# Seven half-sized products for 36 gate-and-up pairs of the second layer (Strassen's identity)

## The chip, the cores and the metric

The kernel runs on one NeuronCore of one Trainium2 chip. The metric is device time in microseconds (us) of one execution; the time given for a kernel is the median of its runs. The profile is of one execution of its own.

TensorE (PE) multiplies a stationary tile of 128 x 128 weights with a moving operand of up to 512 columns and accumulates in PSUM, eight banks of 512 fp32 columns each. PEld is TensorE's weight load, DVE is VectorE, ACT is ScalarE, POOL is GpSimd, SP is SyncE, which only issues transfers here.

## What is computed

A decoder trunk of two layers on 512 tokens of 1024 channels, in fp32. Each layer has three sub-layers, every one with an RMSNorm and a modulation from the conditioning vector: a feed-forward block, a token mixer of three head groups, and a second feed-forward block. Only the feed-forward blocks matter here:

```
def swiglu(h, w_in, w_out):
    gate, up = jnp.split(h @ w_in, 2, axis=-1)
    return (jax.nn.silu(gate) * up) @ w_out

h = modulate(rms_norm(x, norm_g[l, 2]), sh2, sc2)
x = x + FFN_HALF * gt2[:, None, :] * swiglu(h, ffn2_in[l], ffn2_out[l])
```

w_in is 1024 x 5632 (2816 gate and 2816 up columns), w_out 2816 x 1024.

## The kernel before

Channels lie on the 128 partitions, tokens along the free dimension: x is a tile of 8 blocks of 128 channels by 512 tokens. Every fp32 operand of the large products is split in two: a high part, which an ACT copy rounds to TensorE's fp32r type, and a low part, the difference, which one subtraction stores. For the activations these are `hh` and `hl` after the norm (`norm`, lines 333 to 349; its factor `rb` lies in PSUM, x in SBUF) and `gh` and `gl` between the two products of a block; for the weights `whi` and `wlo`. A product of the two is three matmuls (`mm3`, lines 414 to 420): high times high, high times low, low times high, all added up in the same PSUM columns.

A feed-forward block (`ffn`, line 481) works in two halves of 11 pairs each. A pair is the 128 gate columns and the 128 up columns of the same index: one weight tile of 128 x 1024 for each (8 blocks of 128 x 128, along the 1024 input channels). The in-phase of a half runs over its pairs: for each of the two tiles 8 blocks x 3 matmuls of 512 columns into a bank, then `swiglu` (line 540): Silu on ACT out of PSUM, a product with the other bank on DVE, the high part on ACT, the low part on DVE. In the first half the first two pairs go together, in two rounds of 256 tokens, because the norm also comes in two halves of 256 tokens. Behind the in-phase of a half stands its out-phase: 8 output blocks of 33 matmuls each, added to x on DVE (line 426); in the second half ACT and POOL also square and add up x for the next norm (lines 291 to 306).

The weights come through one list, `Weights.units`, that `plan` (line 428) writes in the order of use. `use(i)` (line 181) first advances (line 176) two pointers: tiles up to i+2 are split, in four `whi` and four `wlo` buffers (line 170 on ACT, line 171 on DVE, for a few marked tiles on POOL), and tiles up to i+5 are requested by SP in three `wraw` buffers (line 158). A transfer is issued when its buffer is free, in the order of the list.

While the first layer runs, the 144 tiles of the modulation weights pass through six buffers `adaw` of the same pool as the feed-forward tiles (lines 249 to 260). In the second layer's blocks nothing of that is left to do.

The order of the instructions on each engine is set before the run by a scheduler that works with the order of writing as priority and with estimated times; on the chip each engine works through its list in order.

Lines that matter: 158 load, 170 and 171 high and low part of a weight tile, 418 to 420 mm3, 543 to 546 swiglu, 342 to 349 norm, 301 sums of squares on POOL, 578 to 580 and 590 to 592 and 806, 807, 873 parts of the mixer.

Of the kernel before, what the change touches and what calls it, by code (L numbers as in the profile page):

```python
# [7 lines left out]
F32 = mybir.dt.float32  # L8
# [131 lines left out]
class Weights:  # L140
# [5 lines left out]
        self.units, self.raw, self.hl = [], {}, {}  # L146
        self.nd = self.ns = 0

    def add(self, ap, width, pool=False):
        self.units.append((ap, width, pool))  # L150
        return len(self.units) - 1

    def dma_to(self, i):
        while self.nd < len(self.units) and self.nd <= i:
            ap, w, _ = self.units[self.nd]
            t = self.pool.tile([128, D], F32, name="wraw", tag="wraw", bufs=self.br)
            dst = t[:, :w] if len(ap.shape) == 2 else t[:, :w].rearrange("p (i n) -> p i n", n=ap.shape[2])
            self.nc.sync.dma_start(dst, ap)
            self.raw[self.nd] = t
            self.nd += 1  # L160

    def split_to(self, i):
        while self.ns < len(self.units) and self.ns <= i:
            j = self.ns
            self.dma_to(j)
            _, w, pool = self.units[j]
            r = self.raw.pop(j)
            h = self.pool.tile([128, D], F32R, name="whi", tag="whi", bufs=self.b)
            lo = self.pool.tile([128, D], F32R, name="wlo", tag="wlo", bufs=self.b)
            self.nc.scalar.activation(h[:, :w], r[:, :w], AF.Copy)  # L170
            (self.nc.gpsimd if pool else self.nc.vector).tensor_tensor(lo[:, :w], r[:, :w], h[:, :w].bitcast(F32),  # L171
                                                                       op=ALU.subtract)
            self.hl[j] = (h[:, :w], lo[:, :w])
            self.ns += 1

    def advance(self, i):
        n = 1 if i < KC - 1 else self.AHEAD_SPLIT
        self.split_to(i + n)
        self.dma_to(i + (n if n == 1 else self.AHEAD_DMA))

    def use(self, i):
        self.advance(i)
# [3 lines left out]
class Build:  # L186
    def __init__(self, tc, a, out, dbg=None, layers=L, stop=None):
        self.tc, self.nc, self.a, self.out, self.dbg = tc, tc.nc, a, out, dbg or (lambda *k: None)
        self.layers, self.stop = layers, stop
        self.bgq = []  # L190
        self.nbank = 0
        self.sql = {}

    def bg(self, n=1):
# [11 lines left out]
    def load_consts(self):  # L206
        nc, cp, a = self.nc, self.const, self.a
        self.ones = cp.tile([128, 128], F32, name="ones")
        nc.vector.memset(self.ones, 1.0)
        self.scratch = cp.tile([128, 1], F32, name="scratch")  # L210
        self.eps = cp.tile([128, 1], F32, name="eps")
        nc.vector.memset(self.eps, EPS)

        def ld0(key, shape, dt=F32, eng=None):
            t = cp.tile(shape, dt, name="k_" + key)
            (eng or nc.scalar).dma_start(t, a[key])
            return t

        self.ident = ld0("k_ident", [128, 128])
        self.bada = ld0("bada", [128, L, NADA * KC])  # L220
        self.ng = ld0("ng", [128, L, 3, KC])

        def late():
            def ld(key, shape, dt=F32):
                return ld0(key, shape, dt, nc.gpsimd)

            self.fng = ld("fng", [128, KC])
            self.kd = ld("k_kd", [128, 4])
            self.gc = ld("k_gc", [128, 2])
# [12 lines left out]
            self.onat = cp.tile([128, 4, 2, 256], F32, name="onat")  # L242
            self.sg = cp.tile([128, 4, 2, 256], F32, name="sg")
# [184 lines left out]
    def plan(self):  # L428
        W, a = self.W, self.a
        self.u = {}  # L430
        for l in range(self.layers):
            for which in (0, 1, 2):
                if which != 1:
# [5 lines left out]
                    for half in range(2):  # L439
                        for i in range(FH):  # L440
                            if l == 0 and w == 0 and half == 0 and i < FIRST:
                                continue
                            for s in range(2):
# [37 lines left out]
    def ffn(self, l, which):  # L481
        nc = self.nc
        w = which // 2
        gate = self.mod[l]
        gh = self.gh = self.fp.tile([128, FH, T], F32R, name="gh")
        gl = self.gl = self.fp.tile([128, FH, T], F32R, name="gl", tag="gl")
        for half in range(2):
            i = 0
            if l == 0 and which == 0 and half == 0:
# [2 lines left out]
                self.first_gl = self.last_gl  # L492
                i = FIRST
            while i < FH:
                group = [i, i + 1] if (half == 0 and i == 0) else [i]
                i += len(group)
                js = [(j, s) for j in group for s in range(2)]
# [16 lines left out]
                                     slice(None), k == 0, k == KC - 1)  # L514
                for j in group:
                    self.swiglu(j, ps[j, 0], ps[j, 1])
                self.bg(self.bg_rate * len(group))
            def out_mm(d, p, hs, last):
                for q, (k0, k1) in enumerate(((0, 6), (6, 11))):
# [16 lines left out]
                self.bg(self.bg_rate)  # L536
            if tail:
                self.halves(range(KC - tail, KC), out_mm, gate, 24 * which + 16)

    def swiglu(self, j, pg, pu):  # L540
        nc = self.nc
# [52 lines left out]
    def mixer(self, l):  # L594
# [5 lines left out]
        krot = mp.tile([128, 2, T], F32, name="krot")  # L600
        vnat = mp.tile([128, 4, 256], F32, name="vnat")
        G = mp.tile([128, 120], F32, name="G")[:, 0:96].rearrange("p (c k) -> p c k", c=4)
        onat, sg, stats = self.onat, self.sg, self.stats
        with tc.tile_pool(name="mtmp", bufs=1, reuse_waits="tile") as tp:
            self.tp = tp
# [529 lines left out]
    def open_ffn(self, ada, first=False):  # L1135
        self.fp_cm = self.tc.tile_pool(name="ffn", bufs=1, side="right", reuse_waits="tile")
        fp = self.fp = self.fp_cm.__enter__()
        self.open_sq(fp)
        if ada:
            self.cact = fp.tile([128, D], F32, name="cact")  # L1140
            if first:
# [101 lines left out]
```

## Time and profile before

| | |
|---|---|
| median of 3 runs | 2120.87 us (2117.64 to 2123.96) |
| the profiled execution's own time | 2122.84 us |
| its span, first to last instruction | 2121.1 us |
| PE busy | 2093.0 us (99%) |
| PEld busy | 1743.2 us (82%) |
| DVE busy | 1108.0 us (52%) |
| ACT busy | 796.3 us (38%) |
| POOL busy | 211.0 us (10%) |
| mean granted TensorE clock | 0.996 of 2.4 GHz |
| data moved by DMA | 269.10 MB, mean 127 GB/s |

Busy time is a union: matmuls overlap each other (each is shown some 0.39 us long where one begins every 0.23 us), so the distance of two starts is what a matmul costs. Idle time of an engine that is not the bottleneck costs nothing. In a timeline, the columns are start, length, engine, line, operation, tiles and shape, and in brackets the idle time before it and what ended it.

### The profile page before, as it was taken

How to read it: one execution, taken by the hardware profiler on the slowest of the kernel's cores; microseconds unless marked ns; L12 is line 12 of the kernel's file. 1: busy time of each engine (PE TensorE's matmuls, PEld its weight loads, DVE VectorE, ACT ScalarE, POOL GpSimd, SP SyncE). 2: the span in 40 equal slices, each digit the busy share in tenths (PEclk: the TensorE clock that was granted, in tenths of full speed). 3: DMA queues.
4: the chain of work that ended last, by engine and by line, in shares of the span. 5: the costliest groups of instructions: out<-in, count | busy, mean ns of one | idle time of the engine just before them, and what ended most of it. 6: DMA issues, size and time to landing. Idle time of an engine off the chain costs nothing.

```text
span 2121.1 us, 27803 instructions
## 1 busy us (share of the span) xinstructions
PE 2093.0 (99%) x10938; PEld 1743.2 (82%) x10938; DVE 1108.0 (52%) x1731; ACT 796.3 (38%) x1309; POOL 211.0 (10%) x196
## 2 busy tenths in 40 slices
PE   9999999999999999999999999999999999999998
PEld 7888888988965988888888888889788669888887
DVE  8894333637875799533353333335578754333332
ACT  4422323543665522222342222234527654222323
POOL 1000001312301200000110000012223020000002
PEclk9999999999999999999999999999999999999999
DMA  9894323423310699432333233235232112233322
GB/s 342 310 358 156 91 83 100 144 90 96 96 40 19 236 359 339 159 99 78 91 110 93 82 114 99 75 98 166 82 90 79 31 35 85 91 89 113 96 80 80
DMA packets 93829, 269.10 MB, mean 127 GB/s; under 512 B 10865, under 2 KB 21985, under 8 KB 93698
## 3 DMA queue, kind: packets, MB, share of 16 engines
q1 hardware_dynamic: 92018, 266.06, 38.7%
q8 instruction: 86, 1.41, 0.3%
q0 software_dynamic: 672, 0.58, 0.2%
q10 hardware_dynamic: 1008, 0.69, 0.1%
q14 instruction: 45, 0.37, 0.0%
HBM read 259.94 MB, written 2.10 MB: 124 GB/s over the span
## 4 chain that ended last, share of the span: by engine, by line
PE 96%; DVE 2%; ACT 1%; issue 1%; POOL 0%; DMA 0%; POOLq 0%; DVEq 0%; ACTq 0%
PE mm L418 26%; PE mm L419 26%; PE mm L420 26%; PE o L1062 2%; PE mm L579 1%; PE t L1052 1%; PE mm L578 1%; PE mm L580 1%; PE mm L1020 1%; PE f L419 1%; PE f L418 1%; PE f L420 1%; PE mm L1021 1%; DVE hl L349 0%; PE o L756 0%
## 5 line engine op out<-in xcount | busy, mean ns | idle before, releaser
L170 ACT ACTIVATE whi<-wraw 128x1024 fp32r<-128x1024 f32 (+3 forms) x374 | 361.1, 966 | 1054.8 <-PE mm L419 971.8
L419 PE MATMUL mm<-hl,whi 128*128 128x512 f32 (+1 forms) x1736 | 654.8, 378 | 3.1 <-DVE hl L349 3.1
L420 PE MATMUL mm<-hh,wlo 128*128 128x512 f32 (+1 forms) x1736 | 654.5, 378 | 0.0
L418 PE MATMUL mm<-hh,whi 128*128 128x512 f32 (+1 forms) x1736 | 649.3, 378 | 2.8 <-ACT hh L378 2.2
L171 DVE TENSOR_TENSOR wlo<-wraw,whi 128x1024 fp32r<-128x1024 f32 (+2 forms) x354 | 390.7, 1104 | 447.7 <-ACT whi L170 440.6
L419 PEld LDWEIGHTS mm<-hl,whi 128*128 128x128 f32 x1736 | 328.6, 189 | 62.4 <-DVE hl L349 3.7
L418 PEld LDWEIGHTS mm<-hh,whi 128*128 128x128 f32 x1736 | 326.5, 189 | 64.0 <-issue 3.1
L420 PEld LDWEIGHTS mm<-hh,wlo 128*128 128x128 f32 x1736 | 328.3, 189 | 60.5 <-issue 2.0
L419 PE MATMUL mm<-gl,whi 128*128 128x512 f32 (+1 forms) x792 | 290.2, 366 | 0.0
L420 PE MATMUL mm<-gh,wlo 128*128 128x512 f32 (+1 forms) x792 | 289.6, 366 | 0.0
L418 PE MATMUL mm<-gh,whi 128*128 128x512 f32 (+1 forms) x792 | 289.1, 365 | 0.0
L301 POOL TENSOR_TENSOR sqa<-sqa,sq 128x512 f32<-128x512 f32 (+1 forms) x44 | 51.3, 1165 | 1433.2 <-ACT sq L300 1125.8
L544 DVE TENSOR_TENSOR sg<-sg,mm 128x512 f32<-128x512 f32 x85 | 58.4, 687 | 227.5 <-PE mm L420 225.0
L256 DVE SCALAR_TENSOR_TENSOR adaw<-adaw,cact 128x1024 f32<-128x1024 f32 x144 | 171.7, 1217 | 6.6 <-ACT cact L1150 6.6
L419 PEld LDWEIGHTS mm<-gl,whi 128*128 128x128 f32 x792 | 149.4, 189 | 24.3
L420 PEld LDWEIGHTS mm<-gh,wlo 128*128 128x128 f32 x792 | 149.4, 189 | 24.0
L418 PEld LDWEIGHTS mm<-gh,whi 128*128 128x128 f32 x792 | 149.4, 189 | 24.0
L426 DVE SCALAR_TENSOR_TENSOR x<-mm,mod,x 128x512 f32<-128x512 f32 (+1 forms) x94 | 63.0, 671 | 136.5 <-PE mm L420 136.5
L1027 ACT ACTIVATE p<-mm,nm 128x128 f32<-128x128 f32 (+3 forms) x128 | 66.4, 532 | 18.9 <-DVE nm L1024 18.7
L579 PE MATMUL mm<-wlo,hh 128*128 128x256 f32 x256 | 72.9, 285 | 0.0
L578 PE MATMUL mm<-whi,hh 128*128 128x256 f32 x256 | 72.9, 285 | 0.0
L580 PE MATMUL mm<-whi,hl 128*128 128x256 f32 x256 | 72.7, 284 | 0.0
(289 smaller groups left out, 2145.2 us busy)
## 6 DMA issues: line engine op xcount, KB each, us to landing
wraw<-wfi SPq DMA_DIRECT2D x176, 512.0 KB, 3.7
adaw<-wada SPq DMA_DIRECT2D x144, 512.0 KB, 5.6
wraw<-wfo SPq DMA_DIRECT2D x64, 384.0 KB, 3.1
wraw<-wfo SPq DMA_DIRECT2D x64, 320.0 KB, 2.9
wraw<-wt SPq DMA_DIRECT2D x30, 512.0 KB, 3.7
wraw<-wn SPq DMA_DIRECT2D x16, 512.0 KB, 3.8
w<-w SPq DMA_DIRECT2D x16, 256.0 KB, 5.3
wraw<-wol SPq DMA_DIRECT2D x8, 512.0 KB, 3.7
```

The costliest lines, as they stand in the source:

```text
L170: self.nc.scalar.activation(h[:, :w], r[:, :w], AF.Copy)
L171: (self.nc.gpsimd if pool else self.nc.vector).tensor_tensor(lo[:, :w], r[:, :w], h[:, :w].bitcast(F32), op=ALU.subtract)
L256: i = nc.vector.scalar_tensor_tensor(w, w, 1.0, self.cact, op0=ALU.mult, op1=ALU.mult, accum_out=self.mod[l][:, f:f + 1])
L418: nc.tensor.matmul(out, wh[:, wk], hh[:, hk], start=start, stop=False)
L419: nc.tensor.matmul(out, wh[:, wk], hl[:, hk], start=False, stop=False)
L420: nc.tensor.matmul(out, wl[:, wk], hh[:, hk], start=False, stop=stop)
L426: nc.vector.scalar_tensor_tensor(xd, p, gate, xd, op0=ALU.mult, op1=ALU.add)
L544: nc.vector.tensor_tensor(sg, sg, pu, op=ALU.mult)
L578: nc.tensor.matmul(o, self.hh[:, k, ts], wh[:, cs], start=(k == 0 and c % 2 == 0), stop=False)
L579: nc.tensor.matmul(o, self.hh[:, k, ts], wl[:, cs], start=False, stop=False)
L580: nc.tensor.matmul(o, self.hl[:, k, ts], wh[:, cs], start=False, stop=(k == KC - 1 and c % 2 == 1))
L1027: nc.scalar.activation(p[:, h, :], s[:, i, :], AF.Exp, bias=nm[:, h:h + 1], accum_out=sm[:, h:h + 1])
```

## The change

In the second layer, 36 of the 44 pairs (all but the first four of each block: `seven`) are computed by a variant of Strassen's identity. The pair's weight matrix is seen as four quarters: gate and up, each with the first four and the last four of the 8 input blocks; the activations as four quarters: first and last four input blocks, first and last 256 tokens (A and B). Seven products of a quarter by a quarter, each 4 blocks x 3 matmuls of 256 columns, replace eight. They need sums of weight quarters, made anew for each pair, and sums of activation quarters, made once for a block.

- `Weights.form`: four units a pair, named a, s, c, d, of which only a (gate) and s (up) are loaded. POOL makes the sums, 512 columns each, in place or into one tile `sums`: two for s, one for c, one for d. Each unit is then split as before, d with 512 columns, the others with 1024. The raw tiles of these pairs use the six `adaw` buffers; a transfer is no longer requested while all buffers of its kind are taken.
- `token_forms`: three sums ("1", "2", "4") of four blocks x 256 tokens with high and low parts, on DVE, POOL and ACT, and a fourth ("3"), which is put where `hh` and `hl` of the first four blocks and the last 256 tokens were. They are written in steps behind the first four pairs; the last step, which overwrites, stands in front of the fifth. The tiles are those of the mixer's `onat` and `sg`, which are now allocated by the mixer itself, and those of the squares.
- `seven_products`: four banks a pair (y, x, v, z; all eight banks in turn), the seven products, four adds that fold the banks into one scratch tile r, then Silu, product, high and low part.

```
     def split_to(self, i):
...
-            _, w, pool = self.units[j]
-            r = self.raw.pop(j)
+            _, w, pool, form = self.units[j]
+            r = self.raw.pop(j) if form is None else self.form(j, form)
...
+    def form(self, j, form):
+        nc = self.nc
+        lo, hi = slice(0, T), slice(T, D)
+        if form == "a":
+            return self.raw[j]
+        if form == "s":
+            a, b = self.raw[j - 1], self.raw[j]
+            self.sums = s = self.form_pool.tile([128, D], F32, name="sums", tag="cact", bufs=1)
+            nc.gpsimd.tensor_tensor(s[:, lo], b[:, lo], b[:, hi], op=ALU.add)
+            nc.gpsimd.tensor_tensor(s[:, hi], s[:, lo], a[:, lo], op=ALU.subtract)
+            return s
+        if form == "c":
+            a, b = self.raw[j - 2], self.raw.pop(j - 1)
+            nc.gpsimd.tensor_tensor(b[:, lo], a[:, lo], b[:, lo], op=ALU.subtract)
+            return b
+        a = self.raw.pop(j - 3)
+        nc.gpsimd.tensor_tensor(a[:, hi], a[:, hi], self.sums[:, hi], op=ALU.subtract)
+        return a[:, hi]
...
+        if self.units[i][3] is not None:
+            self.dma_to(i + 2 * self.AHEAD_DMA)
...
+    def seven(self, l, half, i):
+        return l > 0 and (half > 0 or i > 3)
...
+                if self.seven(l, half, i):
+                    if self.tf_steps:
+                        self.form_steps(9)
+                    self.seven_products(l, w, half, i)
...
+                if half == 0:
+                    self.form_steps(len(group))
...
+        def make(name, k0, ts, y):
+            def go():
...
+                for i, eng in enumerate((nc.vector, nc.gpsimd)):
+                    t = self.sc[:, 2 * i:2 * i + 2]
+                    x = [f(v[:, k0 + 2 * i:k0 + 2 * i + 2, ts]) for v in (hh, hl)]
+                    ys = [f(v[:, 2 * i:2 * i + 2, A]) for v in (hh, hl)] if y is None else [f(v[i]) for v in self.last_form]
+                    nc.vector.tensor_tensor(t, x[0], ys[0], op=ALU.subtract)
+                    eng.tensor_tensor(t, t, x[1], op=ALU.add)
+                    eng.tensor_tensor(t, t, ys[1], op=ALU.subtract)
+                    nc.scalar.activation(th[i], t, AF.Copy)
+                    nc.vector.tensor_tensor(tl[i], t, f(th[i]), op=ALU.subtract)
...
+        def three():
+            for k in range(4):
+                t = self.sqp.tile([128, 256], F32, name="hn", tag="hn", bufs=4)
+                nc.vector.tensor_tensor(t, f(hh[:, 4 + k, B]), f(hh[:, k, B]), op=ALU.subtract)
+                nc.vector.tensor_tensor(t, t, f(hl[:, 4 + k, B]), op=ALU.add)
+                nc.vector.tensor_tensor(t, t, f(hl[:, k, B]), op=ALU.subtract)
+                ds.append(t)
+
+        def over():
+            for k in range(4):
+                nc.scalar.activation(hh[:, k, B], ds[k], AF.Copy)
+                nc.vector.tensor_tensor(hl[:, k, B], ds[k], f(hh[:, k, B]), op=ALU.subtract)
+        return [make("1", 0, B, None), make("2", 4, B, "1"), make("4", 4, A, "2"), three, over]
...
+    def seven_products(self, l, w, half, j):
...
+        y, x, v, z = (self.bank8() for _ in range(4))
+        r = self.fp.tile([128, D], F32, name="four", tag="four", bufs=1).rearrange("p (i n) -> p i n", i=4)
+        sg = self.fp.tile([128, T], F32, name="sg", tag="sg", bufs=2)
+        a = use("a")
+        product(y[:, 0], a, 0, "11")
+        nc.scalar.activation(r[:, 1], y[:, 0], AF.Copy)
+        product(x[:, 0], a, T, "21")
+        s = use("s")
+        product(x[:, 1], s, T, "2")
+        nc.vector.tensor_tensor(r[:, 0:4:3], two(r[:, 1]), x, op=ALU.add)
+        product(v[:, 0], s, 0, "1")
+        c = use("c")
+        product(v[:, 1], c, 0, "3")
+        nc.vector.tensor_tensor(r[:, 1:3], two(r[:, 3]), v, op=ALU.add)
+        nc.vector.tensor_tensor(r[:, 3], r[:, 2], v[:, 0], op=ALU.add)
+        product(z[:, 0], use("d"), 0, "22")
+        product(z[:, 1], c, T, "4")
+        nc.vector.tensor_tensor(r[:, 1:3], r[:, 1:3], z, op=ALU.add)
+        nc.scalar.activation(r[:, 0:2], r[:, 0:2], AF.Silu)
+        nc.vector.tensor_tensor(sg.rearrange("p (i n) -> p i n", i=2), r[:, 0:2], r[:, 2:4], op=ALU.mult)
+        nc.scalar.activation(self.gh[:, j, :], sg, AF.Copy)
+        self.last_gl = nc.vector.tensor_tensor(self.gl[:, j, :], sg, self.gh[:, j, :].bitcast(F32), op=ALU.subtract)
```

## Rows read from the trace of the kernel before

**Rows 1.** The page: busy time and share of engines; chain that ended last.
```profile
PE 2093.0 (99%) x10938; PEld 1743.2 (82%) x10938; DVE 1108.0 (52%) x1731; ACT 796.3 (38%) x1309; POOL 211.0 (10%) x196
...
PE 96%; DVE 2%; ACT 1%; issue 1%; POOL 0%; DMA 0%; POOLq 0%; DVEq 0%; ACTq 0%
PE mm L418 26%; PE mm L419 26%; PE mm L420 26%; PE o L1062 2%; PE mm L579 1%; PE t L1052 1%; PE mm L578 1%; PE mm L580 1%; PE mm L1020 1%; PE f L419 1%; PE f L418 1%; PE f L420 1%; PE mm L1021 1%; DVE hl L349 0%; PE o L756 0%
```

**Rows 2.** Busy time by stretch: second layer, nine single pairs of each block.
```profile
core 0: us, PE busy (x) PEld busy (x) DVE busy (x) ACT busy (x) POOL busy (x), PEclk, DMA share, GB/s
...
1091.00:1189.00 98.00, 98.00 (x434) 81.17 (x434) 32.68 (x36) 28.03 (x37) 0.00 (x0) 1.00 0.32 96
...
1774.00:1872.00 98.00, 98.00 (x435) 81.12 (x433) 32.95 (x37) 27.90 (x37) 0.00 (x0) 1.00 0.29 90
```

**Rows 3.** PE timeline in a single pair: two matmuls, 48 apart.
```profile
1129.85 0.39 PE L418 MATMUL mm<-hh,whi 128*128 128x512 f32 x1
...
1140.73 0.39 PE L418 MATMUL mm<-hh,whi 128*128 128x512 f32 x1
```

**Rows 4.** PE timeline in the first group: two matmuls, 50 apart.
```profile
1084.94 0.28 PE L418 MATMUL mm<-hh,whi 128*128 128x256 f32 x1
...
1090.94 0.28 PE L420 MATMUL mm<-hh,wlo 128*128 128x256 f32 x1
```

**Rows 5.** DVE timeline in a single pair.
```profile
1134.88 0.69 DVE L544 TENSOR_TENSOR sg<-sg,mm 128x512 f32<-128x512 f32 x1 [3.37 <-PE mm L420]
1135.67 1.23 DVE L171 TENSOR_TENSOR wlo<-wraw,whi 128x1024 fp32r<-128x1024 f32 x1
1136.82 0.68 DVE L546 TENSOR_TENSOR gl<-sg,gh 128x512 fp32r<-128x512 f32 x1
```

**Rows 6.** ACT timeline in the same pair.
```profile
1129.19 1.06 ACT L170 ACTIVATE whi<-wraw 128x1024 fp32r<-128x1024 f32 x1 [3.83 <-PE mm L419]
1130.15 0.58 ACT L543 ACTIVATE sg<-mm 128x512 f32<-128x512 f32 x1
...
1135.60 0.63 ACT L545 ACTIVATE gh<-sg 128x512 fp32r<-128x512 f32 x1
```

**Rows 7.** DVE timeline in the mixer, instructions one behind the other.
```profile
453.51 1.22 DVE L171 TENSOR_TENSOR wlo<-wraw,whi 128x1024 fp32r<-128x1024 f32 x1
454.64 0.68 DVE L807 TENSOR_TENSOR rq<-rq,ex 128x512 f32<-128x512 f32 x1
455.24 0.69 DVE L805 TENSOR_TENSOR ki<-ki,rk 128x512 f32<-128x512 f32 x1
```

**Rows 8.** DVE timeline in the norm of the second layer.
```profile
1063.44 1.66 DVE L342 SCALAR_TENSOR_TENSOR hn<-x,mod,rb 128x256 f32<-128x256 f32 x4 [1.01 <-PE rb L325]
1065.01 0.48 DVE L426 SCALAR_TENSOR_TENSOR x<-mm,mod,x 128x256 f32<-128x256 f32 x1
1065.41 3.26 DVE L349 SCALAR_TENSOR_TENSOR hl<-hn,mod,hh 128x256 fp32r<-128x256 f32 x2
```

**Rows 9.** POOL timeline at the same place.
```profile
1063.41 2.39 POOL L171 TENSOR_TENSOR wlo<-wraw,whi 128x1024 fp32r<-128x1024 f32 x1 [0.38 <-PE rb L325]
```

**Rows 10.** DVE timeline in the mixer, beside POOL.
```profile
485.83 2.84 DVE L592 TENSOR_TENSOR rq<-rq,sw 128x512 f32<-128x512 f32 x1 [1.18 <-POOL sw L590]
488.71 1.67 DVE L873 TENSOR_TENSOR ex<-rq,k_gq 128x512 f32<-128x512 f32 x1
```

**Rows 11.** POOL timeline at the same place.
```profile
485.76 2.36 POOL L171 TENSOR_TENSOR wlo<-wraw,whi 128x1024 fp32r<-128x1024 f32 x1
488.09 1.74 POOL L590 TENSOR_TENSOR sw<-sw,k_sin 128x512 f32<-128x512 f32 x1
```

**Rows 12.** POOL timeline in an out-phase, a 512-wide instruction alone.
```profile
1392.73 1.29 POOL L301 TENSOR_TENSOR sqa<-sqa,sq 128x512 f32<-128x512 f32 x1 [6.20 <-ACT sq L300]
```

**Rows 13.** DMA issues: tiles, count, KB each, median us to landing.
```profile
wraw<-wfi SPq DMA_DIRECT2D x176, 512.0 KB, 3.7
```

**Rows 14.** Busy time by stretch: end of first group, two single pairs.
```profile
1079.80:1091.10 11.30, 11.30 (x97) 11.30 (x96) 4.87 (x5) 5.95 (x7) 0.51 (x1) 1.00 0.21 61
1091.10:1112.80 21.70, 21.70 (x98) 17.98 (x97) 7.48 (x8) 6.32 (x8) 0.00 (x0) 1.00 0.47 138
```

More of the change, by code (lines that the diff above doesn't have):

```diff
@@ L147, in __init__, with add @@
         self.nd = self.ns = 0
-    def add(self, ap, width, pool=False):
-        self.units.append((ap, width, pool))
+    def add(self, ap, width, pool=False, form=None):
+        self.units.append((ap, width, pool, form))
         return len(self.units) - 1
@@ L154, in dma_to @@
         while self.nd < len(self.units) and self.nd <= i:
-            ap, w, _ = self.units[self.nd]
-            t = self.pool.tile([128, D], F32, name="wraw", tag="wraw", bufs=self.br)
+            ap, w, _, _ = self.units[self.nd]
+            if ap is None:
+                self.nd += 1
+                continue
+            f = self.units[self.nd][3] is not None
+            if sum((self.units[i][3] is not None) == f for i in self.raw) == (6 if f else self.br):
+                break
+            t = self.form_pool.tile([128, D], F32, name="wraw", tag="adaw", bufs=6) if f else self.pool.tile([128, D], F32, name="wraw", tag="wraw", bufs=self.br)
             dst = t[:, :w] if len(ap.shape) == 2 else t[:, :w].rearrange("p (i n) -> p i n", n=ap.shape[2])
@@ L241, in late @@
             nc.gpsimd.memset(self.hv, 0.0)
-            self.onat = cp.tile([128, 4, 2, 256], F32, name="onat")
-            self.sg = cp.tile([128, 4, 2, 256], F32, name="sg")
             self.stats = cp.tile([128, 2, 2, 4, 2], F32, name="stats")
@@ L442, in plan @@
                                 continue
+                            if self.seven(l, half, i):
+                                for s, form in enumerate("ascd"):
+                                    ap = a["wfi"][l, w, half * FH + i, s] if s < 2 else None
+                                    self.u[l, w, "in", half * FH + i, form] = W.add(ap, T if form == "d" else D, form=form)
+                                continue
                             for s in range(2):
@@ L484, in ffn @@
         gate = self.mod[l]
+        self.tf_steps = list(self.token_forms()) if l else []
         gh = self.gh = self.fp.tile([128, FH, T], F32R, name="gh")
@@ L494, in ffn @@
             while i < FH:
+                if self.seven(l, half, i):
+                    if self.tf_steps:
+                        self.form_steps(9)
+                    self.seven_products(l, w, half, i)
+                    i += 1
+                    self.bg(self.bg_rate)
+                    continue
                 group = [i, i + 1] if (half == 0 and i == 0) else [i]
@@ new lines, in bank8, with product, two @@
+    def bank8(self):
+        self.nbank8 += 1
+        return self.pt([128, 2, 256], ("mm", "mm", "mm", "f", "t", "t", "t", "o")[self.nbank8 % 8], name="mm")
+    def seven_products(self, l, w, half, j):
+        nc = self.nc
+        def product(out, wt, c0, form):
+            h = self.tf[form]
+            for k in range(4):
+                self.mm3(out, wt, slice(c0 + 128 * k, c0 + 128 * k + 128), h[k], slice(None),
+                         k == 0, k == 3)
+        def two(t):
+            return t[:, None, :].to_broadcast([128, 2, 256])
+        use = lambda form: self.use(l, w, "in", half * FH + j, form)
+        y, x, v, z = (self.bank8() for _ in range(4))
[20 more added lines that the diff above has]
+        self.last_gl = nc.vector.tensor_tensor(self.gl[:, j, :], sg, self.gh[:, j, :].bitcast(F32), op=ALU.subtract)
@@ L602, in mixer @@
         G = mp.tile([128, 120], F32, name="G")[:, 0:96].rearrange("p (c k) -> p c k", c=4)
+        self.onat = self.const.tile([128, 4, 2, 256], F32, name="onat", tag="onat", bufs=1)
+        self.sg = self.const.tile([128, 4, 2, 256], F32, name="sg", tag="sg", bufs=1)
         onat, sg, stats = self.onat, self.sg, self.stats
@@ L1138, in open_ffn @@
         self.open_sq(fp)
+        self.W.form_pool = fp
         if ada:
```

26 lines of the change are left out of this document (25 added, 1 removed).

## The prediction

> **What bounds the kernel now.** I read the page's shares and its chain of waits first. TensorE is busy for 2093.0 of 2121.1 us, and 96% of the chain that ended last is TensorE, three quarters of it the three matmul lines of mm3 [rows 1]. So time is won only where TensorE gets less to do and nobody else becomes late. Next, the table by stage for the second layer: in the nine single pairs of a first half (98 us, 10.9 each) TensorE never idles, DVE is busy a third, ACT 29%, POOL not at all [rows 2]. The engines that get new work have room there: that is the change's ground. The two feed-forward blocks of this layer hold 44 pairs; 36 are rewritten.
>
> **TensorE's share of the change.** A pair is now 2 weight tiles x 8 blocks x 3 = 48 matmuls, 512 columns wide. Two starts 48 matmuls apart lie 10.88 us apart, 226.7 ns each [rows 3]. The new pair is 7 products x 4 blocks x 3 = 84 matmuls, 256 wide. This width occurs already, in the first group: 50 of them take 6.00 us, 120.0 ns each [rows 4]. 84 x 0.120 = 10.08 us. One product in eight goes, but narrow matmuls carry the same fixed part (2 x 120.0 - 226.7 = 13.3 ns), so the gain is 7%, not 12.5%: 0.80 us a pair, 36 x 0.80 = **-28.9 us**.
>
> The Trainium skill ("TensorE: Matmul & The Clock Gate", Back-to-back issue gap) gives columns / 2.4 GHz + 2.5 ns for a start to start. That would be 215.8 and 109.2 ns, 10.36 against 9.17 us a pair, -42.7 us, and by the rest of this sum about 2088 us. The rows differ from it at both widths, at a granted clock of 1.00 [rows 2], and I go by the rows.
>
> **DVE and ACT.** All durations below are start to start, since consecutive instructions overlap by some 0.08 us. Now a pair costs DVE two low-part subtractions of 1024 (1.15), one product with the up half (512) and one subtraction for gl (512) [rows 5]. A 512 two-input instruction is 0.60, a 1024 one 1.13 [rows 7], a 256 one 0.40 [rows 8]. New pair on DVE: low parts of a, s, c (3 x 1.14) and d (0.60), the adds that fold x, v and z out of PSUM (3 x 0.60) and the 256 one (0.40), the product and gl (1.20). Sum **7.4 us** of 10.08. ACT: three copies of 1024 at 0.96, one of 512, one of 256, Silu, gh [rows 6], at most 0.63 each for the short ones: 5.4 us. Both fit; they cost nothing while they stay covered by TensorE's 10.08.
>
> **POOL.** The weight sums are four 512-wide instructions a pair: two for s, one for c, one for d, 1.29 us each when alone [rows 12], 5.2 us. They run in place on raw tiles, of which six hold three pairs, and a load lands 3.7 us after issue [rows 13]; SP issues as many as before, two a pair, asked for up to ten list entries ahead. So POOL has time too, by itself.
>
> But DVE and POOL get in each other's way. DVE's L592, both inputs in SBUF, started at 485.83 under a POOL instruction that ran 485.76 to 488.12, and took 2.84 us, ending 0.55 after it; the next, L873, took 1.67 under the following POOL one [rows 10, 11]. Four DVE instructions with one input in PSUM ran 1.66 us together under a POOL one of 2.39 and lost nothing [rows 8, 9]. So only DVE work with both inputs in SBUF is shut out. L592 and L873 end 1.71 us apart, against 0.60 unhindered: a POOL sum between two such instructions delays DVE by 1.11. In a new pair six of the ten DVE instructions are of this kind (a, s, c, d, product, gl, 5.2 us); the four PSUM ones (2.2 us) aren't.
>
> DVE's room is 10.08 - 7.4 = 2.7 us. Four sums can take 4 x 1.11 = 4.4 at worst. It fits if at least 1.8 us of them lie under PSUM adds (2.2 us are to be had) or under DVE's two waits inside the closing chain, for Silu (0.58) and for gh (0.63) [rows 6]. In the order written, x stands behind the split of d, v behind that of the next a, z behind that of the next s, three places where a sum can slip under an add; and POOL's sums hang only on raw tiles landed long before (d also on the split of a, whose tile it overwrites), so POOL mostly stands ready. Cost per pair between 0 and 11.8 - 10.08 = 1.7 us; I take 0.1, near the lower end since covers of 3.4 us stand against a need of 1.8: **+3.6 us**. If the cover is gone, the next thing late is a weight split, and TensorE waits for it.
>
> **Waits added.** The copy of y into the scratch tile (one buffer) waits until the previous pair's product has read it, some 2 us into the pair; behind it on ACT stand the high parts of c and d, due at 5.8 and 7.2 us. The add of z waits for the seventh product; behind it on DVE are product, gl and splits due 3 us and more later, and for gl the out-matmuls. The eight banks hold two pairs, so no bank is late. All zero. Moving onat and sg into the mixer issues nothing: zero. The tile loads change buffers, not bytes or order: zero.
>
> **Token sums.** Three sums of 4 x 256 (each six DVE instructions of 0.60, two on POOL, two ACT copies), then twelve of 256 and four more to store: 10.8 + 4.8 + 1.6 = 17.2 us of DVE, 6 x 1.29 of POOL, for each block. The norm's second half leaves DVE by 1079.8; from there to the end of the first group, 1091.1, DVE is busy 4.9 us, and 7.5 in the two single pairs behind it, up to 1112.8, where the seven products start; POOL has 0.5 us in both [rows 14]. The last store is needed 5.8 us later. In these 39 us DVE then has 17.2 + 4.9 + 7.5 and about 6 for the first new pair: 36. POOL's ten sums in the stretch (six here, four for that pair) may add up to 11. So 0 to 8 us a block; I take 3, since half or more of the ten will find DVE in PSUM work or waiting: **+6 us**.
>
> **Sum.** -28.9 + 3.6 + 6.0 = -19.3 against the profiled execution's 2122.84: 2103.5. That execution lies 2.0 over the median of the runs, 2120.87, so against it **2102 us**, 0.9% less. 0.3% of this kernel, 6.4 us, is about what a measurement can tell from no change.
>
> **Rivals.**
> 1. *Slower: DVE and POOL shut each other out.* Order on DVE is fixed before the run. Where it puts subtractions one behind the other with sums waiting, each sum costs 1.11. With one of four under an add (0.60), a pair takes 7.4 + 4.4 - 0.6 = 11.2 us, DVE-bound: 36 x (11.2 - 10.88) = +12, and the token stretch at its bound +8 more for one block: 2133 to 2141 us. It decides from the point where less than 1 us a pair is covered (7.4 + 4.4 - 1.0 = 10.88). For it: L592 and L873, two in a row. Against it: the covers above. All four uncovered would be 11.8, +35 us. The Trainium skill ("SBUF — State Buffer", Who interferes with whom) says that a DVE instruction with two SBUF inputs and a GpSimd one that reads SBUF hold the shared port exclusively for a whole instruction. By that rule the trace agrees: 2.84 instead of 0.69 us, and nothing lost by PSUM readers.
> 2. *Nothing gained.* Cover of about 1 us a pair: 10.9 us, TensorE waits for splits as long as it saves: 2115 to 2127.
> 3. *Token sums late.* The fifth pair waits 8 us in both blocks, pairs then run at 10.08: 2121 - 28.9 + 16 = 2108, up to 2114 with some waits left. For it: 36 us against 39 before any shut-out.
> 4. *TensorE slower at the new products.* If changing banks or waits inside a product cost 0.8 us a pair the gain is gone. Against it: the 50 matmuls of the first group pass from one bank to the next every 24th and keep to 120 ns [rows 4]. I count it within 2.
>
> **How the numbers follow.** Forecast (2091 to 2107, pairs at 10.08 to 10.3): 0.50. Token sums late (2107 to 2114): 0.12. Nothing gained: 0.12. Slower: 0.26. Faster by over 0.3% is the first two, 0.62; same 0.12; slower 0.26. The likeliest case's own range, with its unknown costs at both ends, is 2091 to 2107. For 8 in 10 it reaches over rivals 3 and 2 to rival 1's lower half: 2091 to 2135.
>
> **What would show it.** Right: starts of 256-wide matmuls 120 ns apart and pairs 10.1 us apart, DVE busy over 70% of the stretch, POOL about half; DVE subtractions stretched beyond 1.23 us beside POOL's, yet TensorE without idle time. The token step is right if the fifth pair begins within 3 us of the fourth's end. Rival 1 shows as idle TensorE time ended by the low-part subtraction, several tenths of a us a pair, and a sum over DVE busy near 100%. The forecast is wrong if matmuls of 256 come over 125 ns apart, or if pairs come over 10.6 us apart.

## The result and the profile after

The changed kernel takes **2094.44 us** (median of 4 runs, 2092.16 to 2096.56) beside 2120.52 for the kernel before: a ratio of 0.9876, 95% interval 0.9857 to 0.9895. The forecast was 2102, in the range 2091 to 2135. The profiled execution took 2095.45 us, its span is 2093.7.

The page of the changed kernel, busy time and chain (compare [rows 1]):

```profile
PE 2064.4 (99%) x12234; PEld 1780.8 (85%) x12234; DVE 1365.1 (65%) x2015; ACT 878.9 (42%) x1437; POOL 479.2 (23%) x352
...
PE 93%; DVE 4%; ACT 1%; DMA 1%; issue 1%; POOL 0%; DVEq 0%; SPq 0%; ACTq 0%
```

The two pages already divide the result. TensorE's busy time fell by 2093.0 - 2064.4 = 28.6 us, and its idle time went from 28.1 (2121.1 - 2093.0) to 29.3 us. So the shorter matmul work arrived almost whole, and the waits that the forecast set against it (9.6 us) hardly came.

PE timeline of the changed kernel, two matmuls 84 apart (start, us, engine, line, operation, tiles):

```profile
1139.76 0.28 PE L443 MATMUL mm<-hh,whi 128*128 128x256 f32 x1
...
1149.84 0.28 PE L443 MATMUL mm<-hh,whi 128*128 128x256 f32 x1
```

10.08 us for 84 starts, 120.0 ns each, against 10.88 before [rows 3]. Busy time by stretch, same columns as [rows 2]; norm and first group, the two single pairs, and two stretches of seven-product pairs:

```profile
1066.00:1091.00 25.00, 24.17 (x200) 23.92 (x200) 23.62 (x45) 15.46 (x29) 11.76 (x9) 1.00 0.13 44
1091.00:1113.00 22.00, 22.00 (x101) 18.28 (x100) 21.96 (x23) 10.13 (x18) 13.17 (x8) 1.00 0.24 75
...
1120.00:1180.00 60.00, 60.00 (x502) 60.00 (x502) 59.80 (x62) 30.43 (x43) 40.35 (x24) 1.00 0.34 109
...
1250.00:1350.00 100.00, 100.00 (x836) 100.00 (x835) 91.80 (x100) 52.62 (x70) 62.12 (x36) 1.00 0.23 75
```

Read the first number behind the length (PE) against the third (DVE). In this block TensorE never idles from 1091 on, the fifth pair's start at 1112.4 included. But DVE, a third busy before [rows 2], is now all but full from the norm to 1180: 59.80 of 60 us behind 1120. It is one instruction away from being the bound. How close, one pair of DVE's timeline shows:

```profile
1140.58 0.67 DVE L662 TENSOR_TENSOR four<-four,mm 128x512 f32<-128x512 f32 x1
1141.18 1.72 DVE L177 TENSOR_TENSOR wlo<-sums,whi 128x1024 fp32r<-128x1024 f32 x1
1142.82 0.68 DVE L666 TENSOR_TENSOR four<-four,mm 128x512 f32<-128x512 f32 x1
1143.53 0.42 DVE L667 TENSOR_TENSOR four<-four,mm 128x256 f32<-128x256 f32 x1
1143.87 1.54 DVE L177 TENSOR_TENSOR wlo<-wraw,whi 128x1024 fp32r<-128x1024 f32 x1
1145.33 0.68 DVE L670 TENSOR_TENSOR four<-four,mm 128x512 f32<-128x512 f32 x1
1145.93 1.18 DVE L177 TENSOR_TENSOR wlo<-wraw,whi 128x512 fp32r<-128x512 f32 x1
1147.03 1.78 DVE L672 TENSOR_TENSOR sg<-four 128x512 f32<-128x512 f32 x1
1148.74 1.21 DVE L177 TENSOR_TENSOR wlo<-wraw,whi 128x1024 fp32r<-128x1024 f32 x1
1149.88 0.68 DVE L674 TENSOR_TENSOR gl<-sg,gh 128x512 fp32r<-128x512 f32 x1
1150.48 0.67 DVE L662 TENSOR_TENSOR four<-four,mm 128x512 f32<-128x512 f32 x1
```

and POOL's in the same pair:

```profile
1140.20 1.61 POOL L198 TENSOR_TENSOR wraw<-wraw,sums 128x512 f32<-128x512 f32 x1 [1.83 <-DVE wlo L177]
1143.03 1.29 POOL L190 TENSOR_TENSOR sums<-wraw 128x512 f32<-128x512 f32 x1 [1.22 <-issue]
1144.40 2.16 POOL L191 TENSOR_TENSOR sums<-sums,wraw 128x512 f32<-128x512 f32 x1
1146.52 1.74 POOL L195 TENSOR_TENSOR wraw<-wraw 128x512 f32<-128x512 f32 x1
```

While it is behind, DVE repeats every 9.90 us (1140.58 to 1150.48), 0.18 less than TensorE's 10.08. Its own work is about 7.4; the rest is instructions with both inputs in SBUF stretched beside a POOL sum: s from 1.22 to 1.72, c to 1.54, d from 0.68 to 1.18, the product from 0.68 to 1.78, 2.4 us together. The PSUM adds (L662, L666, L670) stay at 0.67 to 0.68 whatever POOL does.

### The profile page after: what moved, and what is told of

Same layout as the page of the kernel before. It is cut to its first block, busy times and chain, and to the rows that moved or that the text cites. A ratio compares the mean times of both kernels' runs of the same rounds, so it can differ in the third digit from the quotient of the medians.

```text
span 2093.7 us, 31172 instructions
## 1 busy us (share of the span) xinstructions
PE 2064.4 (99%) x12234; PEld 1780.8 (85%) x12234; DVE 1365.1 (65%) x2015; ACT 878.9 (42%) x1437; POOL 479.2 (23%) x352
## 4 chain that ended last, share of the span: by engine, by line
PE 93%; DVE 4%; ACT 1%; DMA 1%; issue 1%; POOL 0%; DVEq 0%; SPq 0%; ACTq 0%
PE mm L443 25%; PE mm L444 25%; PE mm L445 25%; PE o L1200 2%; PE mm L715 1%; PE t L1190 1%; PE mm L714 1%; PE mm L716 1%; PE mm L1158 1%; PE f L444 1%; PE f L443 1%; PE f L445 1%; PE mm L1159 1%; DMA wraw<-wfi 1%; DVE wlo L177 1%
## 5 line engine op out<-in xcount | busy, mean ns | idle before, releaser
L176 ACT ACTIVATE whi<-wraw 128x1024 fp32r<-128x1024 f32 (+4 forms) x410 | 383.1, 935 | 810.7 <-PE mm L444 733.3
L177 DVE TENSOR_TENSOR wlo<-wraw,whi 128x1024 fp32r<-128x1024 f32 (+4 forms) x390 | 441.1, 1132 | 288.3 <-ACT whi L176 284.9
L444 PE MATMUL mm<-hl,whi 128*128 128x512 f32 (+1 forms) x1736 | 593.9, 343 | 2.6 <-DVE hl L374 1.9
L445 PE MATMUL mm<-hh,wlo 128*128 128x512 f32 (+1 forms) x1736 | 593.2, 342 | 0.4 <-DVE wlo L177 0.4
L443 PE MATMUL mm<-hh,whi 128*128 128x512 f32 (+1 forms) x1736 | 588.6, 343 | 2.9 <-ACT hh L403 1.9
L443 PE MATMUL mm<-t,whi 128*128 128x256 f32 x432 | 122.3, 283 | 0.0
L444 PE MATMUL mm<-t,whi 128*128 128x256 f32 x432 | 122.3, 283 | 0.0
L445 PE MATMUL mm<-t,wlo 128*128 128x256 f32 x432 | 122.3, 283 | 0.0
L198 POOL TENSOR_TENSOR wraw<-wraw,sums 128x512 f32<-128x512 f32 x36 | 56.5, 1570 | 190.0 <-DVE wlo L177 190.0
L190 POOL TENSOR_TENSOR sums<-wraw 128x512 f32<-128x512 f32 x36 | 48.2, 1338 | 197.8 <-DVE mod L307 152.0
```

The source lines that it names most:

```text
L190: nc.gpsimd.tensor_tensor(s[:, lo], b[:, lo], b[:, hi], op=ALU.add)
L198: nc.gpsimd.tensor_tensor(a[:, hi], a[:, hi], self.sums[:, hi], op=ALU.subtract)
L443: nc.tensor.matmul(out, wh[:, wk], hh[:, hk], start=start, stop=False)
L444: nc.tensor.matmul(out, wh[:, wk], hl[:, hk], start=False, stop=False)
L445: nc.tensor.matmul(out, wl[:, wk], hh[:, hk], start=False, stop=stop)
```

## The experiments

**1. No weight sums.** All four sums are left out and raw tiles are used in their place, so this kernel computes something else; only its time is read.

```diff
-            nc.gpsimd.tensor_tensor(s[:, lo], b[:, lo], b[:, hi], op=ALU.add)
-            nc.gpsimd.tensor_tensor(s[:, hi], s[:, lo], a[:, lo], op=ALU.subtract)
-            return s
+            return b
...
-            nc.gpsimd.tensor_tensor(b[:, lo], a[:, lo], b[:, lo], op=ALU.subtract)
...
-        nc.gpsimd.tensor_tensor(a[:, hi], a[:, hi], self.sums[:, hi], op=ALU.subtract)
```

> The four weight sums a pair are left out: the seven products take raw weight tiles in their place, so the outputs are not the reference's. POOL does nothing in the seven-product pairs, and DVE's subtractions are no longer stretched. Theory A (TensorE sets the pair at 84 starts of 0.120 us, the sums and what they take from DVE are covered): 2092 to 2096 us, no change against the changed kernel's 2094.4; what can be won is the 2.2 and 3.4 us for which TensorE idles in the two blocks' stretches, and part of that is not the sums' doing. DVE's busy time between 1120 and 1180 falls from 59.8 to about 44 us (7.4 us a pair). Theory B (shutting out still costs, 0.1 us a pair or more as the prediction booked it): 3 us or more faster, 2091 or less.

2093.74 us, 0.9874 (0.9859 to 0.9889), theory A: no difference from the change that these intervals resolve. Busy time by stretch of this kernel:

```profile
1120.00:1180.00 60.00, 60.00 (x502) 60.00 (x501) 45.86 (x60) 31.19 (x42) 0.00 (x0) 1.00 0.31 101
```

DVE falls from 59.80 to 45.86 us and TensorE gains nothing. Over 60 / 10.08 = 5.95 pairs that is 7.7 us of own work a pair (the forecast said 7.4) and 2.3 of shut-out, all of it covered. The run times alone could not tell the 3.6 us that the forecast booked from nothing, their intervals are too wide; the unbroken 60.00 us of TensorE in both kernels can.

**2. The sums on DVE.** In the four lines of experiment 1, gpsimd becomes vector.

> The four sums a pair run on DVE, POOL does nothing there. DVE then has 7.4 + 4 x 0.60 = 9.8 us a pair, against 9.90 measured now with POOL's sums shutting it out. Theory A (the four sums cost DVE about as much from outside, 2.45 us a pair, as they would as its own work, 2.4 us, and both fit under 10.08): 2093 to 2099 us, DVE saturated for about 60 us behind the token sums as now. Theory B (shutting out is what keeps DVE full, its own work would be done sooner): DVE is done with the backlog by 1150 and the time falls to 2092 or less. Theory C (POOL's sums slipped under DVE's work on PSUM and cost it little): DVE falls behind, pairs over 10.2 us for many pairs, 2100 or more.

2096.72 us, 0.9885 (0.9871 to 0.9900), inside theory A; B and C miss. Over the whole execution DVE is busy 1297.3 us without the sums, 1365.1 with POOL's and 1376.6 with its own: the four sums cost it 1.9 us a pair from POOL and 2.2 by its own hand. So moving them to POOL bought DVE almost nothing.

**3. One POOL sum more.** The second half of s is written twice.

```diff
             nc.gpsimd.tensor_tensor(s[:, hi], s[:, lo], a[:, lo], op=ALU.subtract)
+            nc.gpsimd.tensor_tensor(s[:, hi], s[:, lo], a[:, lo], op=ALU.subtract)
```

> One of the four sums is done twice (the second half of s, written again with the same values), five POOL instructions a pair. Theory A (DVE has 0.18 us a pair to spare while it is behind, and each POOL sum between DVE work on SBUF costs it 0.6 to 1.1 us): the pair becomes DVE-bound at 10.5 to 11.0 us, 36 x (0.4 to 0.9) = 15 to 33 us longer: 2109 to 2127 us, with idle TensorE time in front of products. Theory B (the shut-out yields where DVE is behind: sums slip under its work on PSUM, of which 2.2 us a pair is to be had): within 3 us of 2094.4.

**2119.38 us**, 0.9991 (0.9981 to 1.0001): theory A; 25 us lost, nearly the whole gain, by one POOL sum a pair. PE timeline, two pairs (in brackets: idle time before, and what ended it):

```profile
1334.20 0.28 PE L445 MATMUL mm<-hl,whi 128*128 128x256 f32 x1
1335.14 0.39 PE L446 MATMUL mm<-hh,wlo 128*128 128x256 f32 x1 [0.67 <-DVE wlo L177]
...
1345.20 0.28 PE L445 MATMUL mm<-hl,whi 128*128 128x256 f32 x1
1346.14 0.39 PE L446 MATMUL mm<-hh,wlo 128*128 128x256 f32 x1 [0.66 <-DVE wlo L177]
```

A start 0.94 us after the one before it, once a pair, released by a low-part subtraction; pairs 11.00 us apart. DVE and POOL at the same place:

```profile
1331.07 1.78 DVE L673 TENSOR_TENSOR sg<-four 128x512 f32<-128x512 f32 x1
1332.77 2.32 DVE L177 TENSOR_TENSOR wlo<-wraw,whi 128x1024 fp32r<-128x1024 f32 x1
```

```profile
1330.56 1.74 POOL L196 TENSOR_TENSOR wraw<-wraw 128x512 f32<-128x512 f32 x1
1332.26 1.74 POOL L192 TENSOR_TENSOR sums<-sums,wraw 128x512 f32<-128x512 f32 x1
```

The split of a, 1.21 us in the changed kernel, now takes 2.32, and DVE's other instructions of the pair keep their order and their times: the fifth sum costs DVE 1.1 us, the price that the forecast read from [rows 10, 11], and 9.90 + 1.10 = 11.00. Not every pair pays: TensorE has this wait 18 times in the 36 pairs.

**4. Eight half-sized products.** The kernel before, with the same 36 pairs as 96 matmuls of 256 columns and no sums.

```diff
-                        for k in range(KC):
-                            self.mm3(ps[j, s], wt, ...
+                        for hs in (slice(0, 256), slice(256, 512)) if seven else (slice(0, 512),):
+                            for k in range(KC):
+                                self.mm3(ps[j, s][:, hs], wt, ...
```

> The kernel before, with the 36 pairs done as eight products of half the width (96 matmuls of 256 columns in place of 48 of 512), no sums, no change on DVE, ACT and POOL. It prices the width apart from the eighth product. Theory A (a start every 120.0 ns at 256 columns against 226.7 at 512): 36 x (96 x 0.1200 - 48 x 0.2267) = 36 x 0.64 = +23 us on the kernel before, 2143 to 2145 us. Theory B (a narrow matmul costs half a wide one where nothing else is in the way, and the changed kernel's 120 ns is a price of its sums or its changing operands): 2120 to 2126 us.

2144.88 us, 1.0112 (1.0097 to 1.0127); against its own 2121.85 of before that is +23.0, theory A to the tenth. Two starts 96 apart:

```profile
1139.82 0.28 PE L419 MATMUL mm<-hl,whi 128*128 128x256 f32 x1
...
1151.34 0.28 PE L419 MATMUL mm<-hl,whi 128*128 128x256 f32 x1
```

11.52 us, 120.0 ns each. So the change is two steps: halving the width costs 23.0 us, dropping one of eight products returns 12 x 0.120 = 1.44 us a pair, 51.8 us. The formula of the Trainium skill ("TensorE: Matmul & The Clock Gate", Back-to-back issue gap), columns / 2.4 GHz + 2.5 ns, would by an estimate make this run some 4.3 us slower than before (36 pairs, 109.2 and 215.8 ns a start). That section calls it the gap of an isolated matmul; the measured 23.0 decides against it for this stream of them.

**5. DVE's product twice.**

```diff
         nc.vector.tensor_tensor(sg.rearrange("p (i n) -> p i n", i=2), r[:, 0:2], r[:, 2:4], op=ALU.mult)
+        nc.vector.tensor_tensor(sg.rearrange("p (i n) -> p i n", i=2), r[:, 0:2], r[:, 2:4], op=ALU.mult)
```

> Silu's half times the other half is written twice by DVE (same values), 0.60 us more of DVE's own work a pair, POOL as in the changed kernel. Theory A (DVE has at most 0.18 us a pair to spare while it is behind): the pair becomes DVE-bound at 9.90 + 0.60 = 10.5 us, 36 x 0.42 = 15 us longer, 2105 to 2111 us, with idle TensorE time once a pair. Theory B (the additional instruction opens another place under which a POOL sum slips, or DVE's waits take it): within 3 us of 2094.4. Theory C (the additional instruction has both inputs in SBUF and is itself shut out by a sum): 1.1 to 1.7 us a pair, 2117 us or more.

2105.50 us, 0.9927 (0.9910 to 0.9943): +11 us, in theory A's band. DVE's timeline of two pairs, gl to gl:

```profile
1831.06 0.69 DVE L675 TENSOR_TENSOR gl<-sg,gh 128x512 fp32r<-128x512 f32 x1
...
1841.68 0.69 DVE L675 TENSOR_TENSOR gl<-sg,gh 128x512 fp32r<-128x512 f32 x1
```

10.62 us instead of 9.90. A DVE instruction of 0.69 us costs DVE 0.72 a pair here; the POOL sum of experiment 3 cost it 1.10.

**6. Token sums written late.** No step beneath the first four pairs, all in front of the fifth.

```diff
-                if half == 0:
-                    self.form_steps(len(group))
```

> All five steps of the token sums are written in front of the fifth pair, none beneath the first four. The rest is the changed kernel. Theory A (the cover of the first four pairs is what makes the token sums free): the fifth pair waits for about 17 us of DVE's work and its queue, less the 5.8 us before the last sum is needed: 10 us or more a block, 2114 us or more, with one long idle stretch of TensorE at the fifth pair of each block. Theory B (the order on DVE is made from readiness, and the sums are pulled forward wherever they are written): within 3 us of 2094.4, with sums on DVE long before the fifth pair.

2095.02 us, 0.9882 (0.9866 to 0.9899): no change, theory B. The first sum on DVE starts where it did (1075.90 us in the changed kernel):

```profile
1075.97 0.69 DVE L612 TENSOR_TENSOR four<-hh 128x512 f32<-128x512 f32 x1
```

Here the scheduler's order on DVE follows readiness, not the place in the text. The cover lies in how much work stands ahead of the fifth pair, not in where the calls are written.

**7. Seven products from the fourth pair on.** 38 pairs in place of 36, one pair less of cover.

```diff
-        return l > 0 and (half > 0 or i > 3)
+        return l > 0 and (half > 0 or i > 2)
```

> The seven products begin one pair earlier (38 pairs in place of 36), so one pair less covers the token sums. TensorE alone: 2 x 0.80 = 1.6 us less, 2092.8 us. Theory A (DVE is full from the norm until seven pairs behind the token sums, so a pair less of cover is missing): DVE has 7 us less of room, TensorE waits 3 to 7 us a block, 2099 to 2108 us. Theory B (the token sums have room to spare): 2091 to 2094 us.

**2108.97 us**, 0.9946 (0.9931 to 0.9960): 14.5 slower than the change, just past theory A. PE's waits in the second block, 1765 to 1800 (total, times, longest):

```profile
PE mm L444 <- DVE t L618: 5.2, 1, 5.2
PE mm L443 <- ACT t L617: 1.7, 1, 1.7
```

TensorE stands in front of the first new pair until the token sums are stored; the first block has the same 5.2. With four pairs of cover the wait is near nothing, with three 5 to 7 us a block.

**8. The first layer too.** Eleven pairs of the first layer's first block (second half) in seven products, its token sums beneath the first half's pairs, what is left of the modulations issued ahead of the out products.

```diff
+        return half > 0 and w == 0 if l == 0 else half > 0 or i > 3
...
+            while l == 0 and w == 0 and self.bgq:
+                self.bg()
```

> The second half of the first layer's first block, 11 pairs, is done as seven products too, its token sums beneath the pairs of the first half, and what is left of that layer's modulations is issued ahead of the out products. From 180 us on DVE is a third busy there. Theory A (TensorE-bound pairs, covered token sums): 11 x 0.80 = 9 us less, 2084 to 2088 us. Theory B (modulations, token sums and POOL's sums collide on DVE in the first 180 us): a stall of TensorE in front of the out products that eats the gain, 2092 us or more.

2092.84 us, 0.9868 (0.9854 to 0.9883): little of the 9 us, inside theory B. PE's largest wait between 50 and 80 us:

```profile
PE mm L443 <- ACT hh L403: 4.2, 2, 2.6
```

From 20 to 80 us this wait adds up to 8.4 us, and TensorE is busy 52.8 of 60 us, where the changed kernel has 60.00. Token sums had moved into the first 70 us, in between the norm's own work on DVE, and the first products waited for the norm.

**9. The same, token sums held back.** An order-only dependency sets the first instructions of each sum behind the last gl of the first half's pairs.

```diff
+        def held(i):
+            if self.hold:
+                self.tc.add_manual_dep(i.ins, self.hold.ins.name, AFTER, reason="token sums later")
```

> As the run before with 11 pairs of the first layer, but the token sums of that block may not be placed before the last gl of the first half's pairs, so they come beneath the out products, where DVE has little to do. Theory A (the run before lost 6.4 us of TensorE to token sums pulled into the first 80 us, ahead of the norm's work, and would otherwise have had its 11 x 0.80 = 9 us): 2084 to 2088 us, and TensorE without idle time between 50 and 80 us. Theory B (the modulations issued ahead of the out products or POOL's sums cost as much by themselves): 2091 us or more.

2091.52 us, 0.9863 (0.9847 to 0.9880): theory A misses, the time is inside theory B. Nothing idles near 60 us any more, but PE's waits between 20 and 430 us are now

```profile
PE mm L444 <- ACT whi L176: 2.4, 1, 2.4
PE mm L446 <- DVE wlo L177: 1.2, 2, 0.8
```

at 172 to 192 us, among the out products. From 150 to 180 us DVE is busy 30.00 of 30 us there, with the modulations and the sums at once (23.47 in the changed kernel).

**10. Token sums held in the second layer.** The same dependency, there behind the first group's gl.

```diff
+                    if len(group) == 2:
+                        self.hold = self.last_gl
                     self.form_steps(len(group))
```

> The changed kernel, but no token sum may be placed before gl of the second layer's first pair group, about 1100 us in the first block. In the changed kernel they begin at 1075.9 us, beneath the norm's second half. Theory A (what makes them free is that the order on DVE pulls them into the norm and the first group, 25 us earlier than the prediction let them begin): some 10 to 12 us of sums are then missing at the fifth pair, TensorE waits 7 to 12 us a block there: 2108 to 2119 us. Theory B (they fit beneath the single pairs too, or their place on DVE only displaced splits): 2092 to 2098 us.

**2114.39 us**, 0.9971 (0.9961 to 0.9982): in theory A's range, +20. The first sum on DVE begins at 1094.52 instead of 1075.90, and TensorE waits for stored token sums (`t`). Between 1100 and 1200, and between 1770 and 1880:

```profile
PE mm L445 <- DVE t L625: 3.2, 2, 1.9
PE mm L444 <- ACT t L624: 0.9, 1, 0.9
...
PE mm L445 <- DVE t L625: 2.2, 1, 2.2
PE mm L444 <- ACT t L624: 1.9, 1, 1.9
```

So the early start is part of what pays for the sums. But these waits are 4.1 us a block, not the 7 to 12 that theory A named, and 8.2 of the 20 us. In all TensorE idles 10.8 us more than in the changed kernel, and for the same 12234 matmuls it is busy 9.2 us longer (2073.6 us), largely at a lower clock: 0.94 granted from 1740 to 1800 us, where the changed kernel has 1.00 (see the last section). And something more: DVE's timeline of a pair long after the sums, four POOL sums as in the changed kernel:

```profile
1849.50 2.02 DVE L177 TENSOR_TENSOR wlo<-sums,whi 128x1024 fp32r<-128x1024 f32 x1
...
1852.04 2.32 DVE L177 TENSOR_TENSOR wlo<-wraw,whi 128x1024 fp32r<-128x1024 f32 x1
1854.29 1.77 DVE L681 TENSOR_TENSOR gl<-sg,gh 128x512 fp32r<-128x512 f32 x1
1855.98 0.67 DVE L669 TENSOR_TENSOR four<-four,mm 128x512 f32<-128x512 f32 x1
...
1866.95 0.67 DVE L669 TENSOR_TENSOR four<-four,mm 128x512 f32<-128x512 f32 x1
```

10.97 us from add to add instead of 9.90. The instructions are the same; DVE has them in another order, and the sums meet others of them (a and gl at 2.32 and 1.77 instead of 1.21 and 0.68). In the first block's first half the same ten come every 10.5 us; in the second halves DVE keeps up with TensorE's 10.08.

**11. Token sums off POOL.** Their six POOL instructions a block go to DVE.

```diff
-                for i, eng in enumerate((nc.vector, nc.gpsimd)):
+                for i, eng in enumerate((nc.vector, nc.vector)):
```

> The six token-sum instructions that POOL does in each block go to DVE, 6 x 0.60 = 3.6 us more of DVE's own work in a stretch where DVE is full, and six instructions fewer that shut it out. Theory A (a POOL instruction costs a full DVE 0.6 to 1.1 us, as much as or more than the same work on DVE): no change or up to 3 us faster, 2091 to 2096 us. Theory B (POOL's share is covered there): 3 to 4 us of waiting in front of the fifth pair in each block, 2099 to 2103 us.

2094.08 us, 0.9878 (0.9863 to 0.9892): theory A, no change. As in experiment 2, it doesn't matter which of the two engines does the work.

**12. Nine pairs of the first layer.** The modulations keep their pace; the token sums stand behind the fifth residual of the first half's out products.

```diff
+        return half > 0 and w == 0 and i > 1 if l == 0 else half > 0 or i > 3
...
+                if d == 4 and half == 0:
+                    self.after = self.last_residual
...
+                if l == w == 0 and half == 1:
+                    self.hold = self.after
+                    self.form_steps(4)
```

> Nine pairs of the first layer as seven products, the last nine of its first block's second half. The modulations keep their pace beneath the out products, and the token sums may not be placed before the fifth residual of the first half's out products, some 195 us, when the modulations are done. Theory A (the first-layer runs lost TensorE time only because token sums or modulations were moved in front of what TensorE waits for, around 60 us and 172 us): 9 x 0.80 = 7 us less than the changed kernel's 2094.4, 2085 to 2089 us, no idle TensorE time between 50 and 320 us. Theory B (seven products in the first layer cost something in addition, such as raw tiles or POOL's sums): 2091 us or more.

**2084.63 us** (5 runs, 2083.86 to 2086.73), 0.9834 (0.9820 to 0.9847): faster than both kernels. Busy time by stretch:

```profile
150.00:180.00 30.00, 30.00 (x135) 24.82 (x134) 24.38 (x40) 6.36 (x8) 0.00 (x0) 1.00 0.91 314
180.00:240.00 60.00, 60.00 (x333) 52.59 (x332) 57.19 (x68) 23.90 (x34) 29.76 (x18) 1.00 0.34 112
```

TensorE is busy throughout; DVE has the modulations up to 186 us and the token sums from 180 on. The time is just below theory A's 2085 to 2089. The step from 2094.44 is 9.8 us, a little over the 7.2 that nine pairs explain; the two kernels ran beside their own runs of before (2120.52 and 2119.86), and the 2 to 3 us over are within the intervals.

## Why the prediction was right, and which terms were off

**TensorE: right, to 0.3 us.** -28.9 booked, -28.6 in busy time; 120.0 ns a start, and experiment 4 confirms the fixed part per matmul, +23.0 measured for 36 x 0.64.

**DVE and POOL: mechanism and price right, cover misjudged, term too large.** Booked: +3.6 us (0.1 a pair) for the shut-outs. In the traces about 0 came: in the first block no product waits for a split, in the second one waits 0.4 us. But the reason given, covers of 3.4 us against a need of 1.8, was too comfortable. Where DVE is behind, only 4.4 - 2.4 = 2.0 us of the four sums were covered, and it runs 0.18 us a pair ahead of TensorE. The term came out at nothing because the sum still lies under the limit, not because there was room. Nor do the adds stand on DVE where the forecast read them from the order written (x behind the split of d, v behind that of a, z behind that of s): x comes behind gl, v behind the split of s, z behind that of c. Experiment 3 crosses the limit with one more sum.

**Rival 1 was real.** It named 11.2 us a pair; 11.00 (experiment 3) and 10.97 (experiment 10, in one half of a block) were measured, the second with exactly the change's instructions in another order. One of its signs, DVE busy near 100%, came in the changed kernel too; the idle TensorE time did not. The forecast could not tell which order would come out, so that it was the one of 9.90 us was luck as far as the forecast goes. The Trainium skill's rule ("SBUF — State Buffer", Who interferes with whom) says that a DVE instruction with two SBUF inputs contends with a GpSimd one that reads SBUF. These rows agree: SBUF-only subtractions go from 1.21 to 2.32 us, while the adds that take one input from PSUM keep 0.67.

**Token sums: +6 booked, less than 1 came.** The step that failed is the value taken between 0 and 8 us a block. The forecast counted DVE's work, 36 us, against 39, and then took 3 us for shut-outs. DVE did fill the stretch (21.96 of 22 us), shut-outs included, and was just done in time: the first sum began at 1075.90, beneath the norm's second half, where the forecast had DVE taken until 1079.8. How much of the rest is that early start and how much are sums that met no DVE work is not taken apart. In the first block the fifth pair waits for nothing; in the second the trace has 0.4 us of waiting for a weight split. This cost comes abruptly: next to nothing with the early start and four pairs, 5 to 7 us of waits a block with three (experiment 7), 4.1 without the early start (experiment 10), and a lower clock behind them.

**Sum.** -28.9 + 3.6 + 6.0 = -19.3 was forecast; spans show -27.4. The two over-charged terms, 9.6 booked against 1.2 more of idle TensorE time, are the miss of 8 us.

**Rivals 2 to 4.** Nothing gained and TensorE slower at the new products: refuted by the 120.0 ns and the unbroken 60.00 of 60 us. Token sums late: not here, but it is what experiments 7 and 10 became. Of the signs named, all came: pairs 10.08 us apart, DVE over 70% busy, POOL 62 to 67% (somewhat above half), subtractions stretched to 1.54 and 1.72 with no idle TensorE time.

## What to carry to other kernels

When work moves from the bounding engine to others, read not only their busy time but how many microseconds an iteration they still have when they are behind: here 0.18 us of 10.08, and one instruction more took back the gain. Count a sum on POOL like these (512 columns of fp32, all in SBUF) as up to 1.1 us on DVE too, unless it is sure to run beside DVE's PSUM work; and since the order that makes it so is made by the scheduler, look at it before adding anything. Fewer products in narrower matmuls pay by the measured start-to-start time of the narrow form, not by their count.

## What was not expected of the hardware

A wait of TensorE can cost more than its length. In experiment 10, second block, PE's timeline:

```profile
1808.01 0.28 PE L444 MATMUL mm<-t,whi 128*128 128x256 f32 x1
1810.21 0.43 PE L444 MATMUL mm<-t,whi 128*128 128x256 f32 x1 [1.92 <-ACT t L624]
1810.44 0.41 PE L445 MATMUL mm<-t,whi 128*128 128x256 f32 x1
...
1813.64 0.37 PE L445 MATMUL mm<-t,whi 128*128 128x256 f32 x1
```

Behind 1.92 us of idle time, 17 starts come about 0.214 us apart instead of 0.120, the lower of the clock's two levels, 1.2 GHz: 1.6 us more on top of the wait. The granted clock of 1806 to 1815 is 0.81. So a stall in front of a new pair can be paid nearly twice. It fits experiment 7, where the granted clock of 1102 to 1113 us is 0.71: TensorE is busy 2069.9 us, 5.5 more than in the changed kernel, though the two pairs more should have saved 1.6. Not every wait does this. In experiment 10 too, 1.90 us of idle time in front of 1118.44 are followed by starts 0.12 us apart, and the waits of 0.67 us in experiment 3 leave the granted clock of 1250 to 1350 us at 1.00. What decides is not shown.

And identical instructions settled into two different rhythms, 9.90 and 10.97 us a pair on DVE (the changed kernel and experiment 10), by nothing but their order on DVE and which of them POOL's sums met.
